# Layer 1 of a two-layer trunk: high and low part of an activation side by side, two products per k tile in place of three

## The chip, the cores and the metric

One core of a Trainium2 chip runs the whole program. The metric is the device time of one launch in microseconds, the median of several runs. TensorE (PE) multiplies, VectorE (DVE) and ScalarE (ACT) evacuate PSUM and prepare operands, GpSimd (POOL) does a few elementwise steps, SyncE (SP) issues the weight loads.

## What is computed

Two transformer-like layers work on 256 tokens `x` and 256 context tokens; only `x` comes out, so layer 1 carries 256 columns of activations, and the context serves there as keys and values alone.

```python
h = modulate(rmsnorm(x, norm1_g), sh1, sc1)
p = h @ w_in                                  # 1024 -> 7168: u, v, q, k, v, hyena parts, gates
x = x + g1 * merge_branches(p, attn, lp)      # sgu, attention, hyena; gates; w_branch; w_out
h = modulate(rmsnorm(x, norm2_g), sh2, sc2)
a, b = split(h @ ffn_w_up)                    # 1024 -> 2 x 2816
x = x + g2 * ((gelu(conv(a)) * b) @ ffn_w_down)
```

## The kernel before

Activations lie feature-major: one tile has 128 features on the partitions and the tokens along the free axis. Every large product is made in float32r with both operands split in a high and a low part: three products, high weight by low activation (`rl`), high by high (`rh`), low weight by high. ACT casts the high parts of the weights (L248), DVE subtracts for the low ones (L255). In layer 0 a product streams 512 columns (tokens and context), in layer 1 it streams 256.

`mm_k` (L308 to L310) makes the three products of one k tile, into one PSUM tile `mm`; `fm_run` runs it over all k tiles (8 for inputs of 1024 features, 4 for `w_branch`, 12 and 10 for the halves of `ffn_w_down`), then calls the evacuation function, then pumps the side generators. `fm_chunk` makes two such output tiles of 128 features from a weight chunk of 256 columns; `fm_edge` is its form at a stage's edge and takes two tiles side by side (L313 to L316) for the first two of a stage in layer 1.

No scheduler reorders anything: each engine executes in the order in which the program text emits. For one output tile that order is: ACT casts two high weight parts and DVE subtracts two low parts (for a tile that comes three tiles later: `AHEAD` is 6 parts in layer 1, two parts a tile of eight k), PE runs the tile, ACT or DVE evacuates it, and `pump` emits one step of the oldest side generator. Four PSUM tiles `mm` are in use in turn. The side generators are `sgu`, `hyena` and `attention`; `PACE` gives one step for a 256-column tile of eight k, two for a 512-column one.

Layer 1 goes through these stages: u (4 tiles), v; 12 conv tiles for the hyena parts (ACT L973, then DVE L981 and L983), with steps of `sgu` between; q (4 tiles of 256 columns) and k (4 tiles of 512, since the context has keys too), with steps of `hyena` between; v of the attention; 24 gate tiles (ACT tanh, L1049) and 24 branch tiles of four k, mixed, with steps of `attention` between; `w_out` (8 tiles), the second norm, 44 up tiles (half of kind a: ACT L1137, DVE L981, L983, ACT L1140; half of kind b: DVE L1146, ACT L1148, DVE L1150) and 16 down tiles (DVE L1103), the final norm. In the steps of `attention`, `stack` casts keys and queries (ACT L754, L759, L761; DVE L755, L760), `scores` makes the product S (L776), adds the bias on DVE in PSUM (L779), reduces (L783), exponentiates on ACT (L785) and scales on DVE (L788, L789). In `hyena`, Ze and Zo (L634, L635) are followed by products with the spectrum on DVE (L638 to L652), four sums and differences (L657 to L660), and the inverse y (L667) or yT (L681).

Of the kernel before, what the change touches and what calls it, by code (L numbers as in the profile page):

```python
# [94 lines left out]
def trunk_kernel(ctx: ExitStack, tc: tile.TileContext, A: dict, out: bass.AP):  # L95
# [11 lines left out]
    def U(name, dt=F32, n=512):  # L107
        return unit.tile([128, n], dt, tag="u", name=name)

    def fm(name, n, T, dt=F32):  # L110

        if T == 512:
            return [U(name, dt) for _ in range(n)]
        r = []
        for _ in range((n + 1) // 2):
            u = U(name, dt)
            r += [u[:, 0:256], u[:, 256:512]]
        return r[:n]

    def load_x():  # L120
        for k in range(KD):
# [181 lines left out]
    def mm_k(outs, W, R, k, s0, s1, n):  # L303
# [11 lines left out]
        for o, w in zip(outs, W):  # L315
            mm(o, lhsT=w[k][0], rhs=rl, start=False, stop=(k == n - 1))  # L316

    def fm_run(tiles, R, s0, s1, mid=None):

        n = len(R[0])  # L320
        ps = [psm.tile([128, 512], F32, tag="m", name="mm") for _ in tiles]
        for k in range(n):
            mm_k([p[:, 0:s1 - s0] for p in ps], [W for W, _, _ in tiles], R, k, s0, s1, n)
        if mid:
            mid()
        for (_, evac, m), p in zip(tiles, ps):
# [542 lines left out]
    def layer(l):  # L869
# [39 lines left out]

        call(begin)  # L910


        def late(f):

# [18 lines left out]
        def tm_use(c, ntt, dst, func, period=None):  # L933

            def use(piece):
                W = piece(0)
                rh, rl = S["H"]
                for t in range(ntt):
                    ps = psm.tile([128, 512], F32, tag="m", name="mt")
                    o = ps[:, 0:256]  # L940
                    for k in range(KD):
                        wh, wl = W[k]
                        x, y = rh[k][:, t * 128:(t + 1) * 128], rl[k][:, t * 128:(t + 1) * 128]
                        mm(o, lhsT=x, rhs=wl, start=(k == 0), stop=False)  # L944
                        mm(o, lhsT=x, rhs=wh, start=False, stop=False)  # L945
                        mm(o, lhsT=y, rhs=wh, start=False, stop=(k == KD - 1))  # L946
                    act(out=S[dst][t][:, c * 256:(c + 1) * 256], in_=o, func=func)  # L947
                    if (t + 1) % (period or ctl["pace"][2]) == 0:
                        pump()
            return use  # L950
# [46 lines left out]

        def qk_evac(i, c):
            def ev(m, ps, s0, s1):
                for s in range(s1 // 256):  # L1000
                    act(out=S["qk"][s, c * 2 + m][:, i * 256:(i + 1) * 256], in_=ps[:, s * 256:(s + 1) * 256], func=AF.Copy,
                        scale=1.0 if i else HD ** -0.5)
            return ev

        def qkv_chunks():
# [1 line left out]
                S["qk"] = {(s, m): U("qk") for s in range(2) for m in range(4)}  # L1007
                S["va"] = [U("va") for _ in range(4)]
            call(alloc, False)
            for i, c0, segs in ((0, 1024, full), (1, 1536, [(0, 512)])):  # L1010
                for c in range(2):
                    dense(col(c0 + c * 256), KD, 256,
                          late(lambda c=c, i=i, sg=segs: fm_chunk(S["H"], sg, qk_evac(i, c))))
                    if ada_todo:
                        ada(*ada_todo.pop(0))
# [56 lines left out]
        for i in range(len(todo) + LEAD):  # L1072
# [7 lines left out]
            if i >= LEAD:  # L1080
                b, j = todo[i - LEAD]
                wb = A["w_branch"][l, b].rearrange("(k p) n -> p k n", p=128)

                def before(b=b, j=j):
                    if b == ORDER[-1]:
                        if j == 0:
                            S["M"] = [[], []]
                        for i in range(2):
                            S["M"][i] += fm("Mh" if i == 0 else "Ml", 2, T, F32R)
                call(before, False)  # L1090
                dense(wb[:, :, j * 256:(j + 1) * 256], 4, 256, late(lambda b=b, j=j: fm_chunk(S["B"], full, br_evac(b, j))))

# [19 lines left out]
        st2, st3 = [], []  # L1112

        def alloc_h2():
            S["H"] = [fm("hh", KD, T, F32R), fm("hl", KD, T, F32R)]

        for j in range(4):
            if j == 3:
# [6 lines left out]


        def begin2():
            S["mid"] = [[], []]
        call(begin2)

        def a_evac(j):
# [32 lines left out]
        def up_pair(j):  # L1164
            def pre():
                S["a", j] = fm("a", 2, T)
                S["mh", j], S["ml", j] = fm("mh", 2, T, F32R), fm("ml", 2, T, F32R)
                S["mid"][0] += S["mh", j]
                S["mid"][1] += S["ml", j]
# [15 lines left out]

        def alloc_h1():
            if l + 1 < DEPTH:
                NH1[0] = [fm("hh", KD, 512, F32R), fm("hl", KD, 512, F32R)]

        def down_half(k0, k1, last):  # L1190
            def pre():
                S["R"] = [S["mid"][0][k0:k1], S["mid"][1][k0:k1]]
            call(pre)
            st4 = []
            for m in range(KD):
# [8 lines left out]
            def post():  # L1204
                for i in range(k0, k1):
                    S["mid"][0][i] = S["mid"][1][i] = None
                S.pop("R")
            call(post)

# [239 lines left out]
```

## Time and profile before

| | |
|---|---|
| median of 3 runs | 1454.68 us (1453.69 to 1457.19) |
| profiled execution, its own time | 1453.75 us |
| its span in the trace | 1451.7 us |
| granted TensorE clock, mean | 0.995 |
| PE busy | 1412.6 us, 97% |
| DVE busy | 1006.3 us, 69% |
| ACT busy | 666.9 us, 46% |
| layer 1 in the span | about 957 to 1452 us |

About 2 us of the profiled execution lie around the span. Busy time of PE is modelled from pipelined matmuls whose records overlap, so it says little on short stalls; the distance from one start to the next says more. Each row of a timeline gives start, duration, engine, line, operation and operands, and in brackets how long the engine was idle before it and who released it.

### The profile page before, as it was taken

How to read it: one execution, taken by the hardware profiler on the slowest of the kernel's cores; microseconds unless marked ns; L12 is line 12 of the kernel's file. 1: busy time of each engine (PE TensorE's matmuls, PEld its weight loads, DVE VectorE, ACT ScalarE, POOL GpSimd, SP SyncE). 2: the span in 40 equal slices, each digit the busy share in tenths (PEclk: the TensorE clock that was granted, in tenths of full speed). 3: DMA queues.
4: the chain of work that ended last, by engine and by line, in shares of the span. 5: the costliest groups of instructions: out<-in, count | busy, mean ns of one | idle time of the engine just before them, and what ended most of it. 6: DMA issues, size and time to landing. Idle time of an engine off the chain costs nothing.

```text
span 1451.7 us, 22050 instructions
## 1 busy us (share of the span) xinstructions
PE 1412.6 (97%) x8724; PEld 1215.9 (84%) x8724; DVE 1006.3 (69%) x1870; ACT 666.9 (46%) x1368; POOL 89.2 (6%) x96
## 2 busy tenths in 40 slices
PE   6999999999999999999999999999999999999997
PEld 4887777767787889988878778999789899999997
DVE  5666744676775567666887997578767787776575
ACT  4542332434664335533322433465336755665352
POOL 0020201110000000000001220000110000000000
PEclk9999999999999999999999999999999999999998
DMA  9835434233222523244488455545233445556542
GB/s 350 270 130 189 145 129 162 102 115 124 80 88 76 171 97 108 74 159 145 155 265 263 143 174 156 163 142 171 88 117 123 142 158 192 171 175 172 199 143 68
DMA packets 190594, 221.21 MB, mean 152 GB/s; under 512 B 5563, under 2 KB 174556, under 8 KB 185372
## 3 DMA queue, kind: packets, MB, share of 16 engines
q1 hardware_dynamic: 184848, 206.06, 43.0%
q0 software_dynamic: 3344, 10.75, 2.5%
q10 hardware_dynamic: 2300, 3.01, 0.7%
q8 instruction: 68, 1.11, 0.3%
q14 instruction: 34, 0.28, 0.1%
HBM read 216.65 MB, written 1.05 MB: 150 GB/s over the span
## 4 chain that ended last, share of the span: by engine, by line
PE 82%; DVE 9%; DMA 3%; ACT 3%; issue 1%; ACTq 0%; POOL 0%; SPq 0%; DVEq 0%; POOLq 0%
PE mm L308 22%; PE mm L310 22%; PE mm L309 22%; DMA w<-w_in 2%; DVE wp L255 2%; PE mt L944 1%; PE mt L945 1%; PE mt L946 1%; PE pv L813 1%; PE PT L800 1%; DMA aw<-ada 1%; PE S L776 1%; PE ada L379 1%; ACT wp L248 1%; PE Ze L634 1%
## 5 line engine op out<-in xcount | busy, mean ns | idle before, releaser
L308 PE MATMUL mm<-hl,wp 128*128 128x256 f32 (+1 forms) x1476 | 500.5, 339 | 0.8 <-DVE hl L479 0.7
L310 PE MATMUL mm<-hh,wp 128*128 128x256 f32 (+1 forms) x1476 | 491.5, 333 | 0.5 <-DVE wp L255 0.5
L309 PE MATMUL mm<-hh,wp 128*128 128x256 f32 (+1 forms) x1476 | 491.2, 333 | 0.0
L255 DVE TENSOR_TENSOR wp<-w,wp 128x512 fp32r<-128x512 f32 (+1 forms) x576 | 375.3, 695 | 24.3 <-ACT wp L248 21.2
L248 ACT CAST wp<-w 128x512 fp32r<-128x512 f32 (+1 forms) x576 | 321.4, 610 | 94.9 <-DMA w<-ffn_w_down 45.7
L308 PEld LDWEIGHTS mm<-hl,wp 128*128 128x128 f32 x1476 | 280.3, 190 | 37.4 <-issue 6.4
L309 PEld LDWEIGHTS mm<-hh,wp 128*128 128x128 f32 x1476 | 280.4, 190 | 29.4 <-issue 3.1
L310 PEld LDWEIGHTS mm<-hh,wp 128*128 128x128 f32 x1476 | 280.2, 190 | 28.4 <-DVE wp L255 0.7
L308 PE MATMUL mm<-ml,wp 128*128 128x256 f32 (+1 forms) x392 | 125.9, 321 | 0.0
L310 PE MATMUL mm<-mh,wp 128*128 128x256 f32 (+1 forms) x392 | 125.4, 320 | 0.0
L309 PE MATMUL mm<-mh,wp 128*128 128x256 f32 (+1 forms) x392 | 125.3, 320 | 0.0
L401 DVE SCALAR_TENSOR_TENSOR junk<-wn,scb 128x1024 bf16<-128x1024 f32 x64 | 79.2, 1238 | 2.8 <-ACT scb L389 1.4
L308 PEld LDWEIGHTS mm<-ml,wp 128*128 128x128 f32 x392 | 74.7, 190 | 6.0 <-issue 0.8
L309 PEld LDWEIGHTS mm<-mh,wp 128*128 128x128 f32 x392 | 74.7, 190 | 5.4
L310 PEld LDWEIGHTS mm<-mh,wp 128*128 128x128 f32 x392 | 74.7, 190 | 5.4
L1103 DVE SCALAR_TENSOR_TENSOR xT<-mm,mod,xT 128x256 f32<-128x256 f32 x72 | 33.7, 481 | 62.7 <-PE mm L310 61.1
L1137 ACT ACTIVATE a<-mm,prm 128x256 f32<-128x256 f32 (+1 forms) x48 | 30.8, 644 | 88.1 <-PE mm L310 87.0
L944 PE MATMUL mt<-wp,hh 128*128 128x256 f32 x224 | 64.3, 287 | 2.0 <-ACT va L947 1.3
L308 PE MATMUL mm<-bl,wp 128*128 128x512 f32 (+1 forms) x192 | 65.4, 341 | 0.0
L981 DVE SCALAR_TENSOR_TENSOR a<-mm,prm,a 128x255 f32<-128x255 f32 (+1 forms) x48 | 27.9, 582 | 53.2 <-ACT a L1137 53.2
L310 PE MATMUL mm<-bh,wp 128*128 128x512 f32 (+1 forms) x192 | 64.6, 336 | 0.0
L309 PE MATMUL mm<-bh,wp 128*128 128x512 f32 (+1 forms) x192 | 64.6, 336 | 0.0
(623 smaller groups left out, 2041.0 us busy)
## 6 DMA issues: line engine op xcount, KB each, us to landing
w<-w_in SPq DMA_DIRECT2D x56, 1024.0 KB, 5.2
w<-ffn_w_up SPq DMA_DIRECT2D x44, 1024.0 KB, 5.0
wn<-ada_t SPq DMA_DIRECT2D x24, 1024.0 KB, 5.0
wn<-ada_w SPq DMA_DIRECT2D x16, 1024.0 KB, 4.8
w<-w_branch SPq DMA_DIRECT2D x24, 512.0 KB, 3.4
w<-ffn_w_down SPq DMA_DIRECT2D x16, 768.0 KB, 5.1
w<-ffn_w_down SPq DMA_DIRECT2D x16, 640.0 KB, 4.5
aw<-ada SPq DMA_DIRECT2D x32, 256.0 KB, 5.4
```

The source lines that it names most:

```text
L248: nc.scalar.copy(h, src)
L255: vec.tensor_tensor(out=l_, in0=src, in1=spl[st["lo"]][0], op=ALU.subtract)
L308: mm(o, lhsT=wh, rhs=rl, start=(k == 0), stop=False)
L309: mm(o, lhsT=wh, rhs=rh, start=False, stop=False)
L310: mm(o, lhsT=wl, rhs=rh, start=False, stop=(k == n - 1))
L379: mm(ps[32 * j:32 * j + 32, :], lhsT=scc[:, k, :], rhs=v[:, j], start=(k == 0), stop=(k == KD - 1), tile_position=(0, 32 * j))
L401: vec.scalar_tensor_tensor(out=junk, in0=w[:, t * 1024:(t + 1) * 1024], scalar=1.0, in1=scb[m], op0=ALU.mult, op1=ALU.mult, accum_out=mod[ ...
L634: mm(pe, lhsT=fwd(2 * c), rhs=z[0], start=True, stop=True)
L944: mm(o, lhsT=x, rhs=wl, start=(k == 0), stop=False)
L981: vec.scalar_tensor_tensor(out=yv[:, :, 1:256], in0=pv[:, :, 0:255], scalar=w[:, 0:1], in1=yv[:, :, 1:256], op0=ALU.mult, op1=ALU.add)
L1103: vec.scalar_tensor_tensor(out=xs, in0=ps[:, s * 256 - s0:(s + 1) * 256 - s0], scalar=mod[l][:, gate_t + t, s:s + 1], in1=xs, op0=ALU.mult ...
L1137: act(out=y, in_=ps[:, 0:s1 - s0], func=AF.Identity, scale=w[:, 1:2], bias=b)
```

## The change

In layer 1 the two parts of a k tile lie in one buffer of 512 columns, high in the first half and low in the second (`duo`); the old names `S["H"][0][k]` and so on become views of the halves, and for layer 1's first input, whose context segment is kept too, there is one buffer for each segment (`Parted` finds the right one). A third list entry holds the whole buffers. Where it is there and one tile is run, `fm_run` calls `mm_duo`: the high weight streams the whole buffer in one product of 512 columns, the low weight streams the high half in one of 256 into the first half of the PSUM tile. Then ACT copies the second half of the PSUM tile into a new buffer `half` (L353 of the new file), and DVE adds it to the first half in PSUM (L354), before the old evacuation.

116 output tiles go this way: u, the conv tiles, q, the gates, k (which becomes two tiles of one segment each in place of one of 512 columns), six of `w_out`, 42 of up, the 16 of down. The branch tiles, whose input `S["B"]` is still built by `fm`, the token-major tiles (v) and the tiles run in pairs stay as they were. On PE 880 products go.

```diff
+    def duo(name, n, T):
+        u = [[U(name, F32R) for _ in range(n)] for _ in range(T // 256)]
+        r = [[[seg[i][:, 256 * h:256 * h + 256] for seg in u] for i in range(n)] for h in range(2)]
+        return [[v[0] if len(v) == 1 else Parted(v) for v in p] for p in r] + [u]
...
+    def mm_duo(p, W, u, k, n):
+        wh, wl = W[k]
+        if k:
+            mm(p[:, 0:256], lhsT=wl, rhs=u[:, 0:256], start=False, stop=False)
+        mm(p, lhsT=wh, rhs=u, start=(k == 0), stop=(k == n - 1))
+        if k == 0:
+            mm(p[:, 0:256], lhsT=wl, rhs=u[:, 0:256], start=False, stop=False)
+
     def fm_run(tiles, R, s0, s1, mid=None):
 
         n = len(R[0])
         ps = [psm.tile([128, 512], F32, tag="m", name="mm") for _ in tiles]
-        for k in range(n):
-            mm_k([p[:, 0:s1 - s0] for p in ps], [W for W, _, _ in tiles], R, k, s0, s1, n)
+        if len(R) == 3 and len(tiles) == 1:
+            for k in range(n):
+                mm_duo(ps[0], tiles[0][0], R[2][s0 // 256][k], k, n)
+            t = U("half")[:, 0:256]
+            nc.scalar.copy(t, ps[0][:, 256:512])
+            vec.tensor_tensor(out=ps[0][:, 0:256], in0=ps[0][:, 0:256], in1=t, op=ALU.add)
+        else:
+            for k in range(n):
+                mm_k([p[:, 0:s1 - s0] for p in ps], [W for W, _, _ in tiles], R, k, s0, s1, n)
...
+        def parts(name, n):
+            return [fm(name + "h", n, T, F32R), fm(name + "l", n, T, F32R)] if nseg == 2 else duo(name, n, T)
...
-            for i, c0, segs in ((0, 1024, full), (1, 1536, [(0, 512)])):
+            for i, c0, segs in ((0, 1024, full), (1, 1536, full if l == 0 else [(0, 256), (256, 512)])):
...
-            S["H"] = [fm("hh", KD, T, F32R), fm("hl", KD, T, F32R)]
+            S["H"] = parts("h", KD)
...
-                NH1[0] = [fm("hh", KD, 512, F32R), fm("hl", KD, 512, F32R)]
+                NH1[0] = duo("h", KD, 512)
```

Three places show the order of instructions. The first is ACT in the attention stage, at a gate tile whose pumped step stacks keys and queries (`gt` gate, `K_`, `Q_` stacked keys and queries, `wp` weight parts). Before:

```order
L248 CAST wp<-w 128x512 x2
L1049 ACTIVATE gt<-mm 128x256
L754 CAST K__10876<-qk 64x256
L759 CAST Q__10879<-qk 64x256 x2
L761 COPY Q__10879<-Q__10879 64x256
```

After:

```order
L265 CAST wp<-w 128x512 x2
L353 COPY half<-mm 128x256
L1093 ACTIVATE gt<-mm 128x256
L788 CAST K__10781<-qk 64x256
L793 CAST Q__10784<-qk 64x256 x2
L795 COPY Q__10784<-Q__10784 64x256
```

A copy stands ahead of the tanh, and the tanh now waits for DVE's addition. The second place is DVE at three conv tiles (`pc` the convolved hyena part). Before:

```order
L981 SCALAR_TENSOR_TENSOR pc<-mm,prm,pc 128x255
L983 SCALAR_TENSOR_TENSOR pc<-mm,prm,pc 128x255
L255 TENSOR_TENSOR wp<-w,wp 128x512 x2
L981 SCALAR_TENSOR_TENSOR pc<-mm,prm,pc 128x255
L983 SCALAR_TENSOR_TENSOR pc<-mm,prm,pc 128x255
```

After:

```order
L1025 SCALAR_TENSOR_TENSOR pc<-mm,prm,pc 128x255
L1027 SCALAR_TENSOR_TENSOR pc<-mm,prm,pc 128x255
L272 TENSOR_TENSOR wp<-w,wp 128x512 x2
L354 TENSOR_TENSOR mm<-mm,half 128x256
L1025 SCALAR_TENSOR_TENSOR pc<-mm,prm,pc 128x255
L1027 SCALAR_TENSOR_TENSOR pc<-mm,prm,pc 128x255
```

The addition stands between the weight parts and the convolution, which waits for ACT's evacuation, which waits for the addition. The third place is PE at the second k tile, where the hyena's y is made (`y` the inverse transform, `Ze`, `Zo` the next forward one). Before:

```order
L310 MATMUL mm<-hh,wp 128x512
L667 MATMUL y<-P,kst 128x512
L668 MATMUL y<-T,kst 128x512
L667 MATMUL y<-Pp,kst 128x512
L668 MATMUL y<-Tp,kst 128x512
L634 MATMUL Ze<-tm,kst 128x512
L635 MATMUL Zo<-tm,kst 128x512
```

After:

```order
L341 MATMUL mm<-h,wp 128x512
L701 MATMUL y<-P,kst 128x512
L702 MATMUL y<-T,kst 128x512
L701 MATMUL y<-Pp,kst 128x512
L702 MATMUL y<-Tp,kst 128x512
L341 MATMUL mm<-h,wp 128x512
L343 MATMUL mm<-h,wp 128x256
L340 MATMUL mm<-h,wp 128x256
```

Since the k tile is now two tiles of one step each, y stands after its first segment, and the 16 products of the second segment stand between y and the next Ze.

## Rows read from the trace of the kernel before

**Rows 1.** Page: busy time by engine, and the last chain by engine.

```profile
PE 1412.6 (97%) x8724; PEld 1215.9 (84%) x8724; DVE 1006.3 (69%) x1870; ACT 666.9 (46%) x1368; POOL 89.2 (6%) x96
PE 82%; DVE 9%; DMA 3%; ACT 3%; issue 1%; ACTq 0%; POOL 0%; SPq 0%; DVEq 0%; POOLq 0%
```

**Rows 2.** Windows: stretch, length, busy PE, PEld, DVE, ACT, POOL, clock, DMA, GB/s.

```profile
1087.00:1165.00 78.00, 73.41 (x578) 68.72 (x577) 59.76 (x121) 52.34 (x125) 5.05 (x6) 1.00 0.40 129
1262.00:1318.00 56.00, 56.00 (x469) 56.00 (x468) 41.51 (x82) 35.68 (x74) 0.00 (x0) 1.00 0.55 179
```

**Rows 3.** Timeline of PE: start, duration; three stretches of back-to-back products.

```profile
1000.05 0.28 PE L308 MATMUL mm<-hl,wp 128*128 128x256 f32 x1
...
1003.89 0.28 PE L310 MATMUL mm<-hh,wp 128*128 128x256 f32 x1
...
699.67 0.39 PE L308 MATMUL mm<-hl,wp 128*128 128x512 f32 x1
...
703.98 0.39 PE L309 MATMUL mm<-hh,wp 128*128 128x512 f32 x1
...
1184.17 0.63 PE L776 MATMUL S<-K__10884,Q__10887 128*128 128x512 f32 x2
1184.63 0.28 PE L308 MATMUL mm<-bl,wp 128*128 128x256 f32 x1
```

**Rows 4.** Groups by line and shape, layer 1: count, busy us, mean ns.

```profile
L308 PE MATMUL mm<-hl,wp 128*128 128x256 f32 x677 | 192.7, 285 | 0.0
```

**Rows 5.** The same view: PSUM reads by ACT, a PSUM addition by DVE.

```profile
L1049 ACT ACTIVATE gt<-mm 128x256 f32<-128x256 f32 x24 | 9.2, 383 | 7.4 <-PE mm L310 7.4
L779 DVE TENSOR_TENSOR S<-S,bias 128x256 f32<-128x256 f32 x16 | 6.8, 427 | 3.5 <-PE S L776 3.5
L973 ACT ACTIVATE pc<-mm,prm 128x256 f32<-128x256 f32 x12 | 6.8, 565 | 14.7 <-PE mm L310 13.4 <-issue 1.3
```

**Rows 6.** Chain that ended last, at the end of `w_out`.

```profile
1242.46 0.50 DVE xT L1103
```

**Rows 7.** Attention: the chain's shares from 1095 to 1165 us, and timelines of ACT and DVE.

```profile
by line: DVE wp L255 17.6%; ACT wp L248 9.6%; issue 9.1%; DVE mx L783 6.0%; ACTq L733 3.9%; DVE bl L175 3.8%; DVE S L779 3.0%; DVE m L1057 2.8%; ACT PTs L803 2.7%; DVE K__10178 L755 2.5%; DVE Q__10552 L760 2.0%; ACT gt L1049 2.0%; DVE sm L7
...
1124.52 0.37 ACT L1049 ACTIVATE gt<-mm 128x256 f32<-128x256 f32 x1
...
1125.22 0.42 DVE L755 TENSOR_TENSOR K__10549<-qk,K__10549 64x256 fp32r<-64x256 f32 x1 [0.77 <-ACT K__10549 L754]
...
1130.07 0.43 DVE L779 TENSOR_TENSOR S<-S,bias 128x256 f32<-128x256 f32 x1
...
1130.33 0.38 ACT L1049 ACTIVATE gt<-mm 128x256 f32<-128x256 f32 x1
...
1195.75 0.42 DVE L1059 SCALAR_TENSOR_TENSOR gt<-gt,mm 128x256 f32<-128x256 f32 x1 [1.75 <-PE mm L310]
```

**Rows 8.** Timeline of DVE over one conv tile with a step of `sgu`.

```profile
990.88 0.41 DVE L717 TENSOR_TENSOR mixs<-mix,bB 128x256 f32<-128x256 f32 x1
...
991.67 1.28 DVE L255 TENSOR_TENSOR wp<-w,wp 128x512 fp32r<-128x512 f32 x2
992.87 0.48 DVE L981 SCALAR_TENSOR_TENSOR pc<-mm,prm,pc 128x255 f32<-128x255 f32 x1
...
993.78 0.41 DVE L717 TENSOR_TENSOR mixs<-mix,bB 128x256 f32<-128x256 f32 x1
```

**Rows 9.** Hyena: DVE's second sum (timeline), PE's y (chain), PE's longest wait (waits).

```profile
1039.33 0.68 DVE L658 TENSOR_TENSOR T<-yi 128x512 f32<-128x512 f32 x1
...
1040.58 0.86 PE y L667 x2
...
PE yT L681 <- ACT wp L248: 1.8, 1, 1.8
```

**Rows 10.** Timeline of DVE at an up tile of kind b.

```profile
1286.30 0.42 DVE L1146 TENSOR_TENSOR a<-mm,a 128x256 f32<-128x256 f32 x1 [1.32 <-PE mm L310]
1286.64 0.41 DVE L1150 TENSOR_TENSOR ml<-a,mh 128x256 fp32r<-128x256 f32 x1
```

More of the change, by code (lines that the diff above doesn't have):

```diff
@@ L118, in fm, with __init__, __getitem__ @@
         return r[:n]
+    class Parted:
+        def __init__(self, segs):
+            self.segs = segs
+        def __getitem__(self, ix):
+            c = ix[1]
+            i, n = c.start // 256, c.stop - c.start
+            return self.segs[i][:, c.start - 256 * i:c.start - 256 * i + n]
+    def duo(name, n, T):
+        u = [[U(name, F32R) for _ in range(n)] for _ in range(T // 256)]
+        r = [[[seg[i][:, 256 * h:256 * h + 256] for seg in u] for i in range(n)] for h in range(2)]
+        return [[v[0] if len(v) == 1 else Parted(v) for v in p] for p in r] + [u]
     def load_x():
@@ L910, in layer, with gather @@
         call(begin)
+        def parts(name, n):
+            return [fm(name + "h", n, T, F32R), fm(name + "l", n, T, F32R)] if nseg == 2 else duo(name, n, T)
+        def gather(a, b):
+            a[0] += b[0]
+            a[1] += b[1]
+            if len(a) == 3:
+                a[2][0] += b[2][0]
         def late(f):
@@ L936, in use @@
                 W = piece(0)
-                rh, rl = S["H"]
+                rh, rl = S["H"][0:2]
                 for t in range(ntt):
@@ L999, in ev @@
             def ev(m, ps, s0, s1):
-                for s in range(s1 // 256):
-                    act(out=S["qk"][s, c * 2 + m][:, i * 256:(i + 1) * 256], in_=ps[:, s * 256:(s + 1) * 256], func=AF.Copy,
-                        scale=1.0 if i else HD ** -0.5)
+                for s in range(s0 // 256, s1 // 256):
+                    act(out=S["qk"][s, c * 2 + m][:, i * 256:(i + 1) * 256], in_=ps[:, s * 256 - s0:(s + 1) * 256 - s0],
+                        func=AF.Copy, scale=1.0 if i else HD ** -0.5)
             return ev
@@ L1086, in before @@
                         if j == 0:
-                            S["M"] = [[], []]
-                        for i in range(2):
-                            S["M"][i] += fm("Mh" if i == 0 else "Ml", 2, T, F32R)
+                            S["M"] = [[], []] if nseg == 2 else [[], [], [[]]]
+                        gather(S["M"], parts("M", 2))
                 call(before, False)
@@ L1127, in begin2 @@
         def begin2():
-            S["mid"] = [[], []]
+            S["mid"] = [[], []] if nseg == 2 else [[], [], [[]]]
         call(begin2)
@@ L1166, in pre @@
                 S["a", j] = fm("a", 2, T)
-                S["mh", j], S["ml", j] = fm("mh", 2, T, F32R), fm("ml", 2, T, F32R)
-                S["mid"][0] += S["mh", j]
-                S["mid"][1] += S["ml", j]
+                p = parts("m", 2)
+                S["mh", j], S["ml", j] = p[0:2]
+                gather(S["mid"], p)
             call(pre, False)
@@ L1187, in alloc_h1 @@
             if l + 1 < DEPTH:
-                NH1[0] = [fm("hh", KD, 512, F32R), fm("hl", KD, 512, F32R)]
+                NH1[0] = duo("h", KD, 512)
         def down_half(k0, k1, last):
             def pre():
-                S["R"] = [S["mid"][0][k0:k1], S["mid"][1][k0:k1]]
+                S["R"] = [p[k0:k1] for p in S["mid"][0:2]] + [[p[0][k0:k1]] for p in S["mid"][2:]]
             call(pre)
@@ L1206, in post @@
                     S["mid"][0][i] = S["mid"][1][i] = None
+                    for p in S["mid"][2:]:
+                        p[0][i] = None
                 S.pop("R")
```

## The prediction

> **What bounds the kernel now.** I read the page first: PE is busy for 97% of the span, DVE for 69%, ACT for 46%, and 82% of the chain that ended last is PE's [rows 1]. That is a mean, so I asked layer 1 by stretches. In the up tiles PE is busy throughout and DVE for 41.5 of 56 us; in the attention stage PE is busy for 73.4 of 78 us [rows 2]. The chain tells the two apart: from 1095 to 1165 us its shares go to DVE and ACT, with DVE's weight parts first and no group of `mm` products among the first dozen [rows 7]. There DVE runs without a free place, PE follows, and DVE is first seen waiting for PE again at 1195.75 us [rows 7]. So layer 1 has two regimes: stages that PE paces, where shorter products pay, and the stage that DVE and ACT pace together, where every addition on them costs. The change gives to PE and takes from DVE and ACT.
>
> **What goes: products.** In the 256-column stream 32 steps take 3.84 us, 120.0 ns each; in the 512-column stream 19 take 4.31 us, 226.8 ns each [rows 3]. Twice the columns cost 106.8 ns more, so each product has 13.2 ns that don't depend on its columns. Three of 256 cost 360 ns; one of 256 and one of 512 would cost 346.8. The trace shows no such alternation; the nearest are two 512-column products S followed by one of 256, at 0.46 us for the two, 230 ns each [rows 3]. From there the saving is 10 ns; at the other end the product of 256 costs only half of one of 512, 113 ns, and the saving is 20. I take 13.2, since it comes from the same instruction at both widths. How many: 86 tiles of eight k on layer 1's two norms (of their 688 products 677 have a record, [rows 4]), six of `w_out` (48), and 8 x 22 = 176 on the down side: 912 k steps. The 32 k steps of the keys go the other way, three products of 512 (680.4 ns) become two pairs (693.6). The sum is 912 x 13.2 - 32 x 13.2 = 11.6 us of PE time (8.8 to 18), 0.8% at most of the whole if all of it counted.
>
> The Trainium skill (TensorE: Matmul & The Clock Gate, section on the back-to-back issue gap) gives a warm gap of columns / 2.4 + 2.5 ns. By that a product of 256 takes 109 ns, a fixed part is worth only 2.5 ns, and taking 880 of them away would give 2.2 us. The rows here show 120 and 226.8 at full clock, so I keep 13.2; what would follow from the smaller fixed part is a rival below.
>
> **What is added: a copy and an addition on each of 116 tiles.** ACT's read of 256 columns from PSUM takes 383 ns, DVE's addition of 256 columns in PSUM 427 ns [rows 5]; in a stream the next instruction of that size starts after 0.34 us [rows 10]. Where the tile's result is awaited, the two lie in series: 0.38 + 0.43 and two hand-overs of some 0.03 make 0.86 us. No cover is there at two places, the last tile of `w_out` before the second norm, where DVE's evacuation opens a chain that PE waits for [rows 6], and the last down tile before the final norm: 2 x 0.86 = 1.7 us.
>
> **The attention stage.** 14 gate tiles fall into the stretch from 1095 to 1165 us. Before, DVE did nothing for a gate. Now it adds, in order, ahead of the step's scores, and the tanh on ACT waits for that. Where ACT is ahead of DVE, this costs DVE one slot, 0.34 us: six tiles, 2.0 us. Where ACT is the late one, it costs more. At a stacking step DVE waits 0.77 us for the key's cast, which ACT issues right after the tanh at 1124.52 [rows 7]; copy, addition and tanh now stand in series in front of that cast, 0.9 to 1.06 us. At the step after it, DVE's bias addition came at 1130.07, before ACT's evacuation at 1130.33 [rows 7]; now it has to wait for a copy that starts there, ends at 1130.71, and for the addition: 1.03 us. Eight tiles are of these two kinds: 8.0 us. Together +10.0 us, and PE's gain of 112 k steps is lost here. Bounds: 4.8 (14 slots) to 14.4 (all at the dear price). I take the middle because the kind of each tile can be read off the trace.
>
> **The conv tiles and q.** A conv tile's turn on DVE is now a closed loop: addition to ACT's evacuation to L981 (0.43 + 0.03 + 0.57 + 0.03 = 1.06 [rows 5]), convolution 0.91, weight parts 1.20 [rows 8] = 3.17 us, against 8 x 0.3468 = 2.77 us on PE. With a mixing step 0.79 more on DVE [rows 8], 3.96 against about 3.2. Seven and four such tiles lose 2.8 + 3.0 us, and the head of `sgu`, which sat in idle time of DVE, adds an estimated 5. DVE may fall back three tiles (8.3 us) before PE misses a weight part, so PE stalls some 2.4 us; less its gain on 16 tiles (1.7), +0.7 us (-1.7, if the lead covers all, to +4).
>
> **The keys and the hyena.** y moves one segment forward on PE. Before, its operands were ready just in time: the second sum ended at 1040.0, y started at 1040.58 [rows 9]. Three additions in front (1.0 us) put the sums at 1041.0, while PE arrives at about 1038, and a segment of 2.77 us that used to lie before y comes after it. For the second round Ze starts 1.5 us later, and three more additions stand before the sums for yT, which is late by 1.8 us already [rows 9]: +2.1 us at the end (0 to +5; the pumping is finer now, which speaks for the low half).
>
> **What stays hidden.** In the up tiles DVE's loop is 3.17 us for kind a and for kind b 0.46 + 0.34 + 1.20 = 2.0, with 0.33 for the low part L1150 on each b [rows 10]; the mean is 2.75 us, PE's 2.77. The lead of three tiles evens out a and b, and the down tiles between (12 x 0.3468 = 4.2 us on PE, three weight parts on DVE) let DVE catch up. I put 0 here, up to +3 if the mean is a tenth longer. Down, u, the last ten gates and `w_out` have room.
>
> **The sum.** PE's gain counts outside the stretches above: 912 - 112 - 128 = 672 k steps, -8.9. Then +10.0 attention, +0.7 conv and q, +2.1 keys, +1.7 edges: +5.6 us. On the profiled execution (1453.75) that is 1459.4; it lies 0.9 us under the median of 1454.68, so against the median 1460.3. Predicted: 1460.
>
> **Rivals.**
> - *Everything is covered.* The four in-order queues have more slack than their rows show, and only the edges cost: -11.6 + 1.7, 1445 us, up to 1450 if a third of the attention price remains. For it: PE is busy 94% in the attention stage. Against: DVE there waits only for ACT, and PE waits for DVE.
> - *Half of it is covered.* ACT keeps ahead of DVE at all gates (4.8 in place of 10.0) and the lead absorbs conv and keys: -8.9 - 1.7 + 4.8 + 1.7 = -4.1, 1451; with the keys' price 1453.
> - *DVE becomes the bound of the up tiles* (slower still): if the loop of a kind-a tile is not evened out, 21 such tiles lose 0.40 us each against PE, 8.4 us, and the gain of 336 k steps (4.4) is lost: up to 1460 + 8 = 1468. It decides once DVE's mean turn exceeds 2.77 us by more than the lead, 8.3 us over 28 tiles, 0.3 us a tile.
> - *The merged product doesn't save.* With a fixed part of 2.5 to 4 ns, the 672 k steps give 1.7 to 2.7 in place of 8.9: 1466 to 1467.
>
> The Trainium skill's gap rule (same page and section) is that last rival; the spacing of 120 and 226.8 ns in the rows speaks against it.
>
> **Chances.** Forecast 0.55 (1454 to 1466: 0.38 of it over +0.3%, 0.17 within), half covered 0.18 (0.16 within, 0.02 faster), all covered 0.12 (faster), up tiles bound by DVE 0.09, no saving 0.06. Slower by over 0.3% (over 1459.0; 0.3% is about what a measurement of this kernel tells from no change) 0.53, within 0.33, faster 0.14. The range is 1449 to 1470: it leaves out most of the all-covered case and the upper ends of the last two.
>
> **What would show it.** Right: alternating starts of 120 and 227 ns; DVE denser from 1095 us on and the stretch to the last attention step some 10 us longer; PE waiting at y; the up stage shorter by 4 us with PE still back to back. Wrong: waits of PE on L272's weight parts in the up tiles, an attention stage of the same length, or a 256-column product of 109 ns.

## The result and the profile after

The changed kernel takes 1474.31 us (median, 1473.63 to 1476.05), the kernel before 1454.76 us beside it: a ratio of 1.0133, 95% interval 1.0121 to 1.0145. It is 19.6 us slower. I had forecast slower as the likeliest, by 5.3 us, with a range that ended at 1470; the time lies outside it.

The page of the changed kernel, to be held against [rows 1] (busy time by engine, the chain that ended last), and its two new groups of instructions:

```profile
PE 1413.9 (96%) x7844; PEld 1173.2 (80%) x7844; DVE 1047.6 (71%) x1986; ACT 702.5 (48%) x1484; POOL 89.0 (6%) x96
...
PE 76%; DVE 14%; ACT 5%; DMA 2%; issue 2%; POOL 0%; ACTq 0%; SPq 0%; DVEq 0%; POOLq 0%
...
L354 DVE TENSOR_TENSOR mm<-mm,half 128x256 f32<-128x256 f32 x116 | 49.7, 428 | 34.0 <-ACT half L353 33.2
L353 ACT COPY half<-mm 128x256 f32<-128x256 f32 x116 | 42.7, 368 | 40.1 <-PE mm L341 40.1
```

880 products are gone, yet PE is busy for as long as before. DVE has 41 us more work and ACT 36, and PE's share of the chain has fallen by 6 points while those of DVE and ACT have risen by 5 and 2. The group of additions (L354) shows what they take of DVE: 49.7 us of work, and 34.0 us in which DVE stood idle just before one, nearly all of it for the copy on ACT. Only a part of that costs time.

Where the time arises is seen when the same instruction is looked up in both profiles. The traced executions differ by up to 3.9 us before layer 1 begins, where the code is the same. So all such distances, here and below, are counted from the entry into layer 1 (the last product of layer 0), which the profiled execution of the changed kernel reaches 0.07 us after that of the kernel before. Predicted are the running totals of the prediction's own terms.

| place in layer 1 | predicted, running | measured, running |
|---|---|---|
| attention's v tiles (after conv, q, keys, hyena) | +2.4 | +11.2 |
| last gate's tanh | +11.4 | +20.1 |
| first up product (second norm done) | +11.6 | +22.2 |
| final norm (its sum of squares) | +5.6 | +19.9 |

The steps are +2.4, +9.0, +0.2, -6.0 against +11.2, +8.9, +2.1, -2.3. The sum of the attention stage came out as worked out. Three others did not: the stage ahead of it, by 8.8 us, the second norm, and the gain of the up and down tiles.

**The lag.** DVE's timeline at the last conv tiles (start, duration; the idle time in brackets):

```profile
1008.26 0.42 DVE L354 TENSOR_TENSOR mm<-mm,half 128x256 f32<-128x256 f32 x1
1009.32 0.48 DVE L1025 SCALAR_TENSOR_TENSOR pc<-mm,prm,pc 128x255 f32<-128x255 f32 x1 [0.63 <-ACT pc L1017]
...
1011.44 0.42 DVE L354 TENSOR_TENSOR mm<-mm,half 128x256 f32<-128x256 f32 x1
1012.50 0.48 DVE L1025 SCALAR_TENSOR_TENSOR pc<-mm,prm,pc 128x255 f32<-128x255 f32 x1 [0.63 <-ACT pc L1017]
```

A turn takes 3.18 us, the closed loop that the prediction built from [rows 5, 8] (3.17). ACT evacuates the last conv tile (`pc`) 8.6 us later than before; first the row of the kernel before, then of the changed one:

```profile
1012.86 0.57 ACT L973 ACTIVATE pc<-mm,prm 128x256 f32<-128x256 f32 x1 [1.29 <-PE mm L310]
1021.43 0.56 ACT L1017 ACTIVATE pc<-mm,prm 128x256 f32<-128x256 f32 x1 [1.31 <-DVE mm L354]
```

PE has waited for only 1.0 us of the 35 between 980 and 1015, and starts the hyena's first transposes 1.3 us later than before (1016.80 against 1015.53). The lead of three tiles does hide the lag from PE. But it is not gone. In the q tiles ACT and DVE keep each other waiting:

```profile
1026.87 0.39 ACT L353 COPY half<-mm 128x256 f32<-128x256 f32 x1
1027.29 0.43 DVE L354 TENSOR_TENSOR mm<-mm,half 128x256 f32<-128x256 f32 x1 [1.53 <-ACT half L353]
...
1027.76 0.38 ACT L1045 ACTIVATE qk<-mm 128x256 f32<-128x256 f32 x1 [0.50 <-DVE mm L354]
1028.04 1.07 ACT L658 COPY tm<-tp 128x512 f32<-128x512 f32 x2
1028.98 1.16 ACT L265 CAST wp<-w 128x512 fp32r<-128x512 f32 x2
1030.02 0.39 ACT L353 COPY half<-mm 128x256 f32<-128x256 f32 x1
1030.44 0.43 DVE L354 TENSOR_TENSOR mm<-mm,half 128x256 f32<-128x256 f32 x1 [1.53 <-ACT half L353]
```

(Rows of both engines, in order of time; DVE's weight parts are left out.) ACT's copy for the next tile stands behind the evacuation of this one, hyena's two copies and two casts, and that evacuation stands behind DVE's addition: 3.15 us from addition to addition, again more than PE's 2.8 for a tile. So DVE enters the hyena stage 6.6 us late (first P at 1031.81), and then come the keys' additions, in front of y's operands:

```profile
1037.23 0.42 DVE L354 TENSOR_TENSOR mm<-mm,half 128x256 f32<-128x256 f32 x1
...
1041.90 0.42 DVE L354 TENSOR_TENSOR mm<-mm,half 128x256 f32<-128x256 f32 x1
...
1045.36 0.42 DVE L354 TENSOR_TENSOR mm<-mm,half 128x256 f32<-128x256 f32 x1
1045.69 0.68 DVE L691 TENSOR_TENSOR P<-yr 128x512 f32<-128x512 f32 x1
```

PE's waits between 1015 and 1080 us (total, times, longest) show who pays; in [rows 9] there is one of them, 1.8 us at yT:

```profile
PE y L701 <- DVE P L691: 4.7, 1, 4.7
PE yT L715 <- ACT half L353: 2.5, 1, 2.5
PE Ze L668 <- ACT tm L658: 2.2, 2, 1.2
```

What the wait at y does to PE stands in its timeline. First and last product of y, before and then changed:

```profile
1040.41 1.02 PE L667 MATMUL y<-P,kst 128*128 128x512 f32 x2
1042.99 1.02 PE L668 MATMUL y<-Tp,kst 128*128 128x512 f32 x2
```

```profile
1046.52 2.05 PE L701 MATMUL y<-P,kst 128*128 128x512 f32 x2 [4.68 <-DVE P L691]
1050.69 1.02 PE L702 MATMUL y<-Tp,kst 128*128 128x512 f32 x2
```

The 11.2 us at the v tiles add up along PE's timeline. y starts 6.0 us later than before. It then takes 5.0 us in place of 3.4, because the granted clock is at half (1.2 GHz) for 3.4 us from 1046.2 on. The key segment that now stands behind y adds 2.8, and the way from there to the v tiles another 0.8.

**The attention stage.** ACT and DVE at a gate tile whose step stacks keys, in order of time:

```profile
1138.66 0.36 ACT L353 COPY half<-mm 128x256 f32<-128x256 f32 x1
1139.06 0.43 DVE L354 TENSOR_TENSOR mm<-mm,half 128x256 f32<-128x256 f32 x1 [0.45 <-ACT half L353]
1139.52 0.38 ACT L1093 ACTIVATE gt<-mm 128x256 f32<-128x256 f32 x1 [0.50 <-DVE mm L354]
1139.80 0.39 ACT L788 CAST K__10474<-qk 64x256 fp32r<-64x256 f32 x1
...
1140.23 0.42 DVE L789 TENSOR_TENSOR K__10474<-qk,K__10474 64x256 fp32r<-64x256 f32 x1 [0.74 <-ACT K__10474 L788]
```

Copy, addition and tanh stand in series in front of the key's cast, and each engine waits for the other once (0.45 and 0.50 us); DVE's wait for the cast is as it was (0.74 us, 0.77 in [rows 7]). Windows over this stage and over up tiles (length, busy PE, PEld, DVE, ACT, POOL, clock), against [rows 2]:

```profile
1098.00:1184.70 86.70, 75.90 (x470) 65.12 (x469) 63.83 (x136) 57.50 (x140) 4.79 (x6) 0.97 0.37 116
1286.00:1341.00 55.00, 55.00 (x317) 47.97 (x316) 47.76 (x100) 40.31 (x92) 0.00 (x0) 1.00 0.56 182
```

The stage is 8.7 us longer for the same 14 gate tiles. Twice in it, from 1155 and from 1183 us on, the granted clock falls to half for 3.4 us; a run below that has this once shows the stage no shorter. In the up tiles PE has no gap at all.

**Products.** PE's timeline in an up tile:

```profile
1301.00 0.28 PE L340 MATMUL mm<-h,wp 128*128 128x256 f32 x1
1301.12 0.39 PE L341 MATMUL mm<-h,wp 128*128 128x512 f32 x1
1301.35 0.27 PE L340 MATMUL mm<-h,wp 128*128 128x256 f32 x1
1301.46 0.40 PE L341 MATMUL mm<-h,wp 128*128 128x512 f32 x1
...
1302.51 0.39 PE L341 MATMUL mm<-h,wp 128*128 128x512 f32 x1
```

From 1301.12 to 1302.51 four pairs start: 347 ns each by these rounded starts. Over all such pairs between 1262 and 1350 us the start after a product of 256 follows 116.3 ns later and after one of 512 233.9 ns later: 350.2 ns a pair against 3 x 120.0 = 360 before. The saving is 9.8 ns a k step, not 13.2, because in the mixed stream the product of 512 takes 7 ns longer than in the stream of its own kind [rows 3], and the one of 256 only 4 less.

The Trainium skill (TensorE: Matmul & The Clock Gate, section on the back-to-back issue gap) gives columns / 2.4 + 2.5 ns as the gap of an isolated product at full clock; from this follow, as an estimate, 215.8 and 109.2 ns and a saving of 2.5 ns. It says itself that a stream of weight loads and products does not keep to it, which the prediction left out. This trace shows more of each, and four times that saving; the measurement decides.

**The second norm.** The chain at `w_out`'s last tiles:

```profile
1259.16 1.20 DVE wp L272 x2
1260.36 0.35 DVE mm L354
1260.74 0.49 DVE xT L1146
1261.32 0.43 ACT sqt L472
1261.77 0.43 DVE sqt L477
1262.19 1.21 DVE wp L272 x2
```

No product stands in it: a turn of weight parts, addition, residual, square and sum of squares takes 3.03 us, against 2.80 for PE's eight pairs. `w_out` had been paced by PE and is now paced by DVE.

### The profile page after: what moved, and what is told of

Read it like the earlier page. It is cut to its first block, busy times and chain, and to the rows that moved or that the text cites. A ratio compares the mean times of both kernels' runs of the same rounds, so it can differ in the third digit from the quotient of the medians.

```text
span 1471.6 us, 20492 instructions
## 1 busy us (share of the span) xinstructions
PE 1413.9 (96%) x7844; PEld 1173.2 (80%) x7844; DVE 1047.6 (71%) x1986; ACT 702.5 (48%) x1484; POOL 89.0 (6%) x96
## 4 chain that ended last, share of the span: by engine, by line
PE 76%; DVE 14%; ACT 5%; DMA 2%; issue 2%; POOL 0%; ACTq 0%; SPq 0%; DVEq 0%; POOLq 0%
PE mm L325 15%; PE mm L327 15%; PE mm L326 15%; PE mm L341 10%; PE mm L340 5%; DVE wp L272 3%; PE mt L988 1%; PE mt L990 1%; PE mt L989 1%; PE pv L847 1%; ACT wp L265 1%; DVE mm L354 1%; DMA aw<-ada 1%; PE PT L834 1%; PE S L810 1%
## 5 line engine op out<-in xcount | busy, mean ns | idle before, releaser
L325 PE MATMUL mm<-hl,wp 128*128 128x512 f32 (+1 forms) x756 | 292.0, 386 | 0.8 <-DVE hl L513 0.7
L327 PE MATMUL mm<-hh,wp 128*128 128x512 f32 (+1 forms) x756 | 284.8, 377 | 0.5 <-DVE wp L272 0.5
L326 PE MATMUL mm<-hh,wp 128*128 128x512 f32 (+1 forms) x756 | 284.4, 376 | 0.0
L341 PE MATMUL mm<-h,wp 128*128 128x512 f32 x752 | 265.4, 401 | 1.8 <-ACT gt L1093 1.8
L340 PE MATMUL mm<-h,wp 128*128 128x256 f32 x658 | 184.4, 280 | 0.0
L325 PEld LDWEIGHTS mm<-hl,wp 128*128 128x128 f32 x756 | 142.5, 188 | 34.7 <-issue 5.5
L326 PEld LDWEIGHTS mm<-hh,wp 128*128 128x128 f32 x756 | 142.5, 189 | 27.3 <-issue 2.6
L327 PEld LDWEIGHTS mm<-hh,wp 128*128 128x128 f32 x756 | 142.4, 188 | 27.0 <-DVE wp L272 0.7
L341 PEld LDWEIGHTS mm<-h,wp 128*128 128x128 f32 x752 | 137.9, 189 | 29.7 <-ACT gt L1093 2.3
L340 PEld LDWEIGHTS mm<-h,wp 128*128 128x128 f32 x658 | 124.9, 190 | 4.1
L325 PE MATMUL mm<-ml,wp 128*128 128x512 f32 (+1 forms) x216 | 76.2, 353 | 0.0
L327 PE MATMUL mm<-mh,wp 128*128 128x512 f32 (+1 forms) x216 | 75.7, 350 | 0.0
L326 PE MATMUL mm<-mh,wp 128*128 128x512 f32 (+1 forms) x216 | 75.7, 350 | 0.0
L354 DVE TENSOR_TENSOR mm<-mm,half 128x256 f32<-128x256 f32 x116 | 49.7, 428 | 34.0 <-ACT half L353 33.2
```

Source lines behind the costliest of these rows:

```text
L325: mm(o, lhsT=wh, rhs=rl, start=(k == 0), stop=False)
L326: mm(o, lhsT=wh, rhs=rh, start=False, stop=False)
L327: mm(o, lhsT=wl, rhs=rh, start=False, stop=(k == n - 1))
L340: mm(p[:, 0:256], lhsT=wl, rhs=u[:, 0:256], start=False, stop=False)
L341: mm(p, lhsT=wh, rhs=u, start=(k == 0), stop=(k == n - 1))
L354: vec.tensor_tensor(out=ps[0][:, 0:256], in0=ps[0][:, 0:256], in1=t, op=ALU.add)
```

## The experiments

All are built from the changed kernel, unless it says otherwise, and were timed against the kernel before on the same chip. "Old path" means three products of 256 columns and no copy or addition, over the views of the halves.

**Products alone.** `fm_run` without

```diff
-            t = U("half")[:, 0:256]
-            nc.scalar.copy(t, ps[0][:, 256:512])
-            vec.tensor_tensor(out=ps[0][:, 0:256], in0=ps[0][:, 0:256], in1=t, op=ALU.add)
```

> The changed kernel without the copy and the addition at evacuation: each tile's evacuation reads the first half of its PSUM tile alone, so the product of the high weight with the low activation is left out of the result. Everything else, the merged products and the split of the key tiles too, is as changed. Theory: a product has a fixed part of 13.2 ns whatever its columns, 880 fewer give 11.6 us where nothing else is late; y of the hyena, moved forward by the key split, gives back 1 to 2 us. Expected 1443 to 1446 us against 1454.7. Rival, fixed part of 2.5 ns: 2.2 us less products and the same y, 1453 to 1455.

Measured 1449.56 us, ratio 0.9965 (0.9952 to 0.9978): 5.5 us below before, between the two expectations, as the 9.8 ns want it. In its trace the up and down tiles give 5.1 us up to the final norm (512 k steps x 9.8 ns are 5.0), the attention stage nothing: it ends as late as it began (+0.9 us at its first gate, +1.0 at its fourteenth, against before). So the copies and additions, with the waits and clock that follow from them, cost 1474.3 - 1449.6 = 24.7 us, for 116 of them, 0.21 us each on average, and no product saved in the attention stage counts. Both are as the prediction had them in kind. Nor do the products before the hyena count: the last q tile is 1.5 us early, the v tiles 0.3 late.

**Up and down alone.** The first norm's parts, M and the keys as in the kernel before.

```diff
-            for i, c0, segs in ((0, 1024, full), (1, 1536, full if l == 0 else [(0, 256), (256, 512)])):
+            for i, c0, segs in ((0, 1024, full), (1, 1536, [(0, 512)])):
...
-                        gather(S["M"], parts("M", 2))
+                        gather(S["M"], [fm("Mh", 2, T, F32R), fm("Ml", 2, T, F32R)])
...
-                NH1[0] = duo("h", KD, 512)
+                NH1[0] = [fm("hh", KD, 512, F32R), fm("hl", KD, 512, F32R)]
```

> Merged products, copy and addition in the up and down tiles alone; layer 1's first norm output and the input of w_out keep their separate buffers and their three products. Theory (PE paces these stages and DVE just keeps up): 512 k steps at 13.2 ns save 6.8 us, the end of the last down tile costs 0.9: -5.9, 1448.8 us. Rival (DVE becomes the bound of the up tiles): the 336 up steps give nothing and kind a tiles lose up to 0.4 us each: 1452 to 1461 us.

Measured 1451.89 us, ratio 0.9975 (0.9966 to 0.9985). From the entry into layer 1 its trace gains 4.1 us. 512 k steps x 9.8 ns are 5.0, less 0.86 for the last tile before the final norm: 4.2. At 13.2 ns it would be 5.9. That bears out the price of a pair, and that the additions in the up tiles are hidden.

**Conv tiles old.**

```diff
-                dense(col(2560 + c * 256), KD, 256, late(lambda c=c: fm_chunk(S["H"], full, hy_evac(c))))
+                dense(col(2560 + c * 256), KD, 256, late(lambda c=c: fm_chunk(S["H"][:2], full, hy_evac(c))))
```

> The changed kernel, but the 12 conv tiles ahead of the hyena run the three old products without copy and addition. Theory A (what DVE falls behind in the conv tiles is carried under its lead of three tiles into the hyena, where PE waits for DVE's own results, and comes due there): the evacuation of q, 8 to 9 us late in the changed kernel, is on time again, and some 6 to 8 us of the 19.6 go: 1466 to 1468 us. Theory B, that of the prediction (each stage pays its own price, the conv tiles 0.7 us, and the hyena is late by its own additions and the moved y): 1473 to 1474 us.

Measured 1466.08 us, ratio 1.0077 (1.0058 to 1.0097): 8.2 us given back, where the prediction's term for conv tiles and q together was 0.7. Its four times lie between 1463.3 and 1469.9 us, so the 8.2 are good to some 3 us. PE's wait at y falls from 4.7 to 2.5 us, and the attention's v tiles stand 3.7 us after before instead of 11.2.

**Gate tiles old.** The same edit in the call of `gate_evac`.

> The changed kernel, but the 24 gate tiles run the three old products without copy and addition. Theory: the attention stage is paced by DVE and ACT, 14 gates there cost 10 us, ten outside gain 1.1: about 9 us less, 1465 to 1466 us. Two half-clock stretches inside the attention stage of the changed kernel, of 3.4 us each, should go with them. Rival (the attention stage starts late because of the hyena and its own price is small): within 3 us of 1474.

Measured 1466.96 us, ratio 1.0079 (1.0062 to 1.0096): 7.4 us given back. In its trace the distance to before stays within 11.3 to 11.6 us from the first gate to the last, where it grows by 8.3 in the changed kernel. From there to the first up product it loses 3.0 us, the changed kernel 2.1, so a part is lost again at `w_out`. The two stretches at half clock are gone from the stage, as expected. They are not what it costs: with conv tiles old there is one in place of two, and from the first gate to the fourteenth the stage grows by 10.0 us, in the changed kernel by 9.0.

**q and keys old.** The same edit in the call of `qk_evac`; the order of the segments stays.

> The 4 tiles of q and the 8 of the keys go back to three 256-column products and no addition; the order of the segments (y one segment earlier) stays as in the changed kernel. The keys then cost 720 ns a k step in place of 350 x 2. Theory A (the additions themselves load DVE, whose lag of some 8 us from the conv tiles comes due at y and yT): 12 additions of 0.34 to 0.43 us are gone, of which those of the keys stand between the lag and the operands of y and yT; the stall at y (4.85 us) falls to about 2 to 3, and the time to 1470 to 1471 us. Theory B (it is y's move one segment forward that costs; the additions ride along): the stall at y stays above 4 us and the time is 1473.5 to 1475, since 96 k steps lose their saving of 10 ns.

Measured 1467.95 us, ratio 1.0087 (1.0073 to 1.0101): 6.4 us given back, more than theory A said. PE's waits:

```profile
PE y L701 <- DVE P L691: 2.6, 1, 2.6
PE yT L715 <- DVE P L691: 1.1, 1, 1.1
```

In its q tiles the lag shrinks by about 1.8 us a tile (8.4 us at the last conv tile, 1.2 at the last q tile); in the changed kernel it is still 7.9 there.

**Conv, q and keys old together.**

> Conv tiles, q and keys on the old path together, the rest as in the changed kernel. Each alone gave back 8.2 and 6.4 us. Theory A (one shared lag: the conv tiles put DVE 8 us behind, and it comes due at y and yT only because the additions of q and the keys keep DVE from catching up): the two gains overlap; the attention's v tiles stand within 1 us of the kernel before, 11 us are given back and not 14.6: 1463 to 1464 us. Theory B (two separate prices, each at its own place): 1459 to 1460.5.

Measured 1463.68 us, ratio 1.0067 (1.0053 to 1.0080): 10.6 us given back, not the 14.6 that the two gave one by one. The attention's v tiles stand within 0.3 us of before; each alone brought them 7.5 and 6.7 us nearer, together more than the 11.2 there are. So there is one lag, which is built in the conv tiles, kept by the additions of q and the keys, and paid at y and yT: theory A. No stretch at half clock is left between 1040 and 1085 us, so the clock's part comes back with the lag's.

**y's move alone.** The kernel before, with its keys in two segments on the old path (and the offsets in `qk_evac` that go with them).

```diff
-            for i, c0, segs in ((0, 1024, full), (1, 1536, [(0, 512)])):
+            for i, c0, segs in ((0, 1024, full), (1, 1536, full if l == 0 else [(0, 256), (256, 512)])):
```

> The kernel before with one thing of the change alone: layer 1's keys in two segments of 256 columns on the old path, so that y comes one segment earlier on TensorE; no merged product, no addition. The keys' products cost 32 k steps x (720 - 680) = 1.3 us more. Theory A (the move itself costs nothing beyond the products, since DVE has y's operands ready in time when no addition stands before them): at most +1.3 us, 1455 to 1456.5 us, PE's wait at y under 1 us. Theory B (y's operands are just in time in the kernel before, so the move alone makes PE wait for them, as I predicted): a wait of 1 to 2.5 us at y and 1457 to 1459 us.

Measured 1455.35 us, ratio 1.0006 (0.9997 to 1.0016): no difference. Its waits:

```profile
PE y L667 <- DVE P L657: 1.3, 1, 1.3
PE yT L681 <- DVE P L657: 1.1, 1, 1.1
```

The wait at y is there, as theory B said, and yT starts 1.8 us later than before. But the wait at yT is 1.1 us in place of 1.8 [rows 9], the 3.4 us at half clock that the kernel before has from 1062 us on do not occur, and the v tiles come only 0.2 us later. The time is theory A's, though not by its reason: the move costs 1.8 us up to yT, nearly the prediction's 2.1 for keys and hyena, and the clock gives nearly all of it back here.

**`w_out` old.** M's parts apart again (the second hunk of the up-and-down edit). The expectation counts eight tiles; two of them run as a pair and were never merged, so it is six.

> The 8 tiles of w_out go back to the old path (M's parts apart again, no additions); everything else as in the changed kernel. Theory A (with the addition DVE's turn of a w_out tile is 2.98 us against PE's 2.8: 1.20 weight parts, 0.36 addition, 0.50 residual, 0.43 square on ACT, 0.43 sum of squares; so w_out's second half is paced by DVE, the second norm opens late and PE's clock falls for 10 us in place of 3.4): without the addition the turn is 2.6 us, PE paces again, first up tile some 2 to 3 us earlier and the half-clock stretch there back to 3.4 us: 1469.5 to 1471 us. Theory B (only the last addition of 0.86 us lies on the path, as I predicted): 1473.5 to 1474.5.

Measured 1472.12 us, ratio 1.0108 (1.0093 to 1.0124): 2.2 us given back, between the two. In the trace, from the last gate to the first up product, it is 3.1 us, and PE paces `w_out` again (the distance to before is the same from its first tile to its last). But the half clock at the norm did not go back to 3.4 us: it lasts 6.8.

**PE kept busy at the second norm.** Products that nobody reads, written to the sum's PSUM tile ahead of it, 18, 4 and 6 of them at three places.

```diff
+    def fill(n):
+        f = ctl.get("fill")
+        if f:
+            for _ in range(n):
+                mm(f[2][:, 0:f[1].shape[1]], lhsT=f[0], rhs=f[1], start=True, stop=True)
```

> The changed kernel with 28 products of 512 columns whose results nobody reads, put on TensorE where it waits for the second norm of layer 1: 18 before the sums of squares, 4 before and 6 after the broadcast of the root, at most 6.4 us of work in 6.9 us of waiting. Theory A (the 10.24 us at half clock from 1268 us on follow from TensorE's waiting there, and the part of it that lies over the up tiles' first products costs about half of 6 us): the granted clock stays at full, first up tile where it was, the products after it some 3 us earlier: 1471 to 1472 us. Theory B (the first up tiles wait for DVE's norm outputs anyway, so that the clock costs nothing there): 1474 to 1475.

Measured 1472.92 us, ratio 1.0119 (1.0106 to 1.0133). By the times alone the 1.4 us are not settled, since the intervals overlap. The windows at the norm and over the first up products, of the changed kernel and then of this one:

```profile
1266.00:1272.00 6.00, 2.12 (x6) 1.31 (x6) 2.73 (x8) 2.42 (x6) 0.00 (x0) 0.67 0.32 112
1272.00:1279.00 7.00, 6.80 (x34) 6.80 (x35) 6.64 (x17) 4.64 (x10) 0.00 (x0) 0.55 0.00 1
```

```profile
1269.70:1275.70 6.00, 5.65 (x30) 4.76 (x29) 2.81 (x8) 2.54 (x6) 0.00 (x0) 1.00 0.34 119
1275.70:1282.70 7.00, 7.00 (x54) 6.68 (x54) 6.67 (x16) 5.06 (x11) 0.00 (x0) 1.00 0.01 4
```

With PE busy the clock stays at full, and 54 products run in the seven microseconds where 34 ran. The first up product comes when it did, and from the first evacuated up tile to the last down tile everything comes 2.3 us earlier: theory A, by the trace.

**PE kept busy in the hyena stage.** Ten such products before y, five before yT.

```diff
+                        for _ in range(10 if l == 1 and e == 0 else 0):
+                            mm(ps, lhsT=fwd(0), rhs=z[0], start=True, stop=True)
```

> The changed kernel with products whose results nobody reads in TensorE's two waits of the hyena stage, 10 before y (4.3 us of the 4.85 us wait) and 5 before yT (2.2 of 2.65 us). Theory A (the 3.41 us at half clock behind each of the two waits stretch work on the path): the stretches at 1046 and 1073 us go, the attention's v tiles come 1.5 to 3.5 us earlier against the entry into layer 1, 1471 to 1473 us. Theory B (DVE's lag sets the times there, and the clock only rides along): no change, 1473.5 to 1475; if the fillers hold up y, up to 1476.

Measured 1473.96 us, ratio 1.0137 (1.0123 to 1.0151): no change. One window of the changed kernel (PE alone: length, busy, clock) and one of this run (all engines), then PE's rows at y in this run, whose trace enters layer 1 2.1 us later:

```profile
1045.00:1050.00 5.00, 3.48 (x5) 0.66 0.30 103
```

```profile
1045.00:1050.00 5.00, 5.00 (x13) 2.28 (x12) 4.96 (x9) 1.74 (x5) 0.00 (x0) 1.00 0.64 210
```

```profile
1043.74 8.74 PE L702 MATMUL y<-tm,kst 128*128 128x512 f32 x20
1052.32 1.02 PE L703 MATMUL y<-P,kst 128*128 128x512 f32 x2
```

The clock is at full, and the v tiles stand 12.2 us after before, no earlier than the 11.2. But that decides nothing, because the fillers were too long. Each shows as two products of 0.43 us, so the ten took 8.6 us where the wait was 4.7, and y started 3.7 us later than in the changed kernel; yT too. This is the third case of the expectation. From yT's start to the v tiles 2.8 of these 3.7 us were made up with the clock at full, so the clock is not without a price here.

Three other runs show that price, since their code up to the v tiles is that of the changed kernel: gates old, `w_out` old, and fillers at the second norm. In all four the q tiles end 7.8 to 7.9 us late, and the v tiles come the later the longer the half clock lasted between 1040 and 1090 us: +11.0 and +11.2 us with 6.8 us of it, +11.6 with 10.2, +12.8 with 13.7. So the lag is DVE's, it makes PE wait, and the half clock after the waits adds to it.

**A faster version.** Merged products in up and down alone, the last down tile on the old path, and fillers at the second norm.

```diff
-                      late(lambda m=m, ev=ev: fm_edge(S["R"], halves, ev, 1, st4, 4, before3) if last and m >= 4 else
+                      late(lambda m=m, ev=ev: fm_edge(S["R"][:2] if m == 7 else S["R"], halves, ev, 1, st4, 4, before3) if last and m >= 4 else
```

> Towards a better version: merged products only in up and down (the first norm's parts and M as in the kernel before), the last down tile before the final norm on the old path, and 28 products of 256 columns whose results nobody reads in PE's waits at the second norm. From 1451.9 us (merged products in up and down alone): the end edge gives back 0.4 to 0.9, the clock at the second norm 1 to 1.7: 1449.3 to 1450.5 us. If the half clock of 3.4 us at the second norm costs nothing, 1451 to 1451.5; if the waits there get longer by the fillers, 1452 to 1453.

Measured 1449.20 us (1447.67 to 1450.22), ratio 0.9956 (0.9943 to 0.9968): faster than both kernels, 5.9 us below before. The fillers have no part in it by the trace: the clock stays at full at the norm, but the first up product comes 1.0 us later than in the run of up and down alone, and from the first up tile to the last but one of down the two stay within 0.1 us of each other. The last down tile gives 0.9 us, and the final norm behind it 0.4 more; the rest of the 2.7 us between the two medians is not in these traces. Then with four products before yT, of the kind used in the hyena stage:

> As the run with merged products in up and down alone, the last down tile old and fillers at the second norm (1449.2 us), with 4 more products that nobody reads before yT, where TensorE waits for 1.95 us and 3.4 us at half clock follow. If the clock then stays at full: 1.2 to 1.7 us less at the attention's v tiles, and of it what the DVE-paced attention stage doesn't take back: 1447.5 to 1449 us. If the attention stage takes all of it or the fillers hold up yT: 1449 to 1450.

Measured 1449.26 us, ratio 0.9964 (0.9952 to 0.9977): the same time. The stretch of half clock behind yT is gone: between 1060 and 1065 us the granted clock is 1.00, against 0.77 in the run without these four. The four took 3.4 us where the wait was 1.8, so that yT started 1.5 us later; still the v tiles come 1.2 us earlier, and the last down tile 1.6. The medians don't show it: the five times of this run spread over 1.2 us, those of the run without them over 2.6. What becomes of the gain stays open.

## Why the prediction was wrong

- **Products (-8.9).** The count was right, and so was where they count (nothing in the attention stage). The size was off: 672 x 9.8 ns = 6.6 us at most. I computed the mixed stream from two uniform ones, though I had named the row that was nearer, two products S and one of 256, with 10 ns. That row was right. Missed: 2.3 us.
- **Attention (+10.0).** Right in its sum: less the gain of the ten later gates it was +9.0, and the trace has +8.9; 7.4 in the time when the gates went back. That eight tiles cost some 1.0 us and six 0.34 was not checked tile by tile.
- **Conv tiles and q (+0.7), keys and hyena (+2.1).** This is the step that failed: together +2.8 was forecast, and 10.6 us came back with the three kinds of tile. The turn of 3.17 us was right, the lag near (2.8 + 3.0 + 5 us against 8.5), and PE did stall little there. But I then let the rest of the lag vanish because PE did not see it. The lead of three tiles covers what PE needs from DVE for its next weights. It doesn't cover results, and hyena asks for results. I also put no loss on the q tiles, where the loop of ACT and DVE (3.15 us) gives DVE no room to catch up, and added the keys' three slots to an unlagged start. y's move, which I priced with them, did cost 1.8 us up to yT when it was made alone. And the wait at y brought the half clock, which made y 1.6 us longer; I had no term for that.
- **`w_out` has room.** Wrong: with the addition its turn is 3.03 us on DVE. I gave the edge 0.86 less 0.6; the trace says 2.1 us at the first up product. The other edge was too cheap as well: the old path at the last down tile gave 0.9 us there and 0.4 in the final norm, against 0.86.
- **The clock.** The prediction has no term for it. In the changed kernel the half clock at the second norm lasts 10.2 us in place of 3.4, mostly over up tiles; filling PE's waits gave 2.3 us in the trace. That up and down gave 2.3 us in place of 6.0 has three parts: the smaller saving (512 x 3.4 ns = 1.7), the first up tile, which falls back another 1.2 us at half clock, and 0.6 in the final norm.
- **Up tiles (0).** Right: PE 55.00 of 55 us busy, DVE 47.76. The rival in which DVE becomes their bound is refuted, and so are "everything covered" and "half covered". Of the rival of the fixed part a third held: 3.4 of the 13.2 ns were not there, where it took away 9 to 11.

Each undone by itself, the three account for the loss: 10.6 (conv, q, keys) + 7.4 (gates) + 2.2 (`w_out`) = 20.2 us from 1474.3 gives 1454.1; the run of up and down alone, in which all three and u are old, has 1451.9. That the three add up was not tested by undoing them one on top of the other, and the last 2 us were not taken apart.

## What to carry to other kernels

A lag that a lead hides is not gone: follow it past the end of the stage, to the first place where another engine asks for a result and not for prefetched operands, and price it there. Trading a few nanoseconds of each product for a copy and an addition on two other engines pays only where the product's engine paces and nobody awaits the tile, here in up and down. Where the first engine waits just ahead of a dense stretch, work that nobody reads can keep its clock up; but look in the trace whether it fits into the wait, for here it held up y by 3.7 us in one run and the first up product by 1.0 in another, and the gain was gone.

## What the hardware showed that I had not expected

- A product's spacing depends on its neighbours: 256 columns 120.0 ns among their like and 116.3 behind one of 512; 512 columns 226.8 among their like and 233.9 behind one of 256.
- The granted clock fell to half (1.2 GHz) after stretches in which PE waited (4.7 us before y in the changed kernel), though not after all of them (with y's move alone, waits of 1.3 and 1.1 us left it at full), and PE's unread products in those waits kept it at full (2.4 GHz) at all the places where they were put: the second norm, y and yT. It was worth 2.3 us of the trace at the changed kernel's second norm, where the half clock lasted 10.2 us, and nothing at the faster version's, where 3.4 us of it went and the fillers came out 1.0 us too long.
